# Weight, x and work tiles of a hybrid decoder layer laid on one grid of 512 bytes

## The chip, the cores and the metric

The kernel runs on one core of a Trainium2 chip. The metric is the time of one execution on the device, in microseconds. A core has five engines that run beside each other and meet through semaphores: TensorE (PE in the profile; PEld is its weight loading), VectorE (DVE), ScalarE (ACT), GpSimd (POOL) and SyncE (SP), which here only issues transfers. Engines work on SBUF, a memory of 128 partitions; a tile takes the same range of bytes in every partition, so the place of a tile is one start address, and addresses below are bytes within a partition. Products leave TensorE into PSUM.

## The reference

One decoder layer for 256 tokens of 2048 channels in float32: half a SwiGLU, a mixer of attention heads and S5 state-space channels side by side, half a SwiGLU again, and a last norm.

```python
h = h + 0.5 * swiglu(rmsnorm(h, ffn1_norm[l]), ffn1_w1[l], ffn1_w3[l], ffn1_w2[l])
proj = rmsnorm(h, mix_norm[l]) @ w_in[l]
...
a = nsa_mixer(q, kc, vc, ksl, vsl, kw, vw, gates, rel_bias, ...)
s = s5_mixer(u_ssm, ...)
h = h + jnp.concatenate([a, s], axis=-1) @ w_out[l]
h = h + 0.5 * swiglu(rmsnorm(h, ffn2_norm[l]), ffn2_w1[l], ffn2_w3[l], ffn2_w2[l])
return rmsnorm(h, final_norm)
```

Here swiglu(x) = (silu(x @ w1) * (x @ w3)) @ w2 with 5632 hidden columns. Its three matrices in two half-steps are most of the 337 MB that the layer reads, and most of its products.

## The kernel before

**Three passes for a float32 product.** A float32 number is split into hi (12 significant bits, type float32r) and lo (the rest). A product of x and w is three float32r matmuls that add up in PSUM: x hi with w hi, x hi with w lo, x lo with w hi. A matmul has a stationary operand, loaded as 128 x 128 weights into the array, and a moving operand that streams through it, here up to 512 columns.

**Row products** (`gemm_rows`, L173 to L175) have 128 tokens of x as the stationary operand (xh, xl) and 512 columns of the weight matrix as the moving one (whi, wlo); one k-tile of 128 rows takes 2 token tiles x 3 passes = 6 matmuls. For the product with w2 the hidden activations are the stationary operand; they lie in work tiles (wk). **Column products** (`cols_step`, L184 to L186) are the other way round: 128 columns of the weight are stationary and the 256 tokens move.

**Weights** arrive by two k-tiles: `wload` (L143) has SP load 512 KB into a raw tile, and `wtiles` (L151) splits it with one ScalarE instruction (L121, hi) and one VectorE instruction (L122, lo) into tiles whi and wlo, three buffers of each. After each pair of k-tiles `tick` advances the side work (S5 parameters, scan, attention) by a step. Instructions run on every engine in the order in which the program issues them, apart from a priority for the splits.

**Half-step** (`ffn`, L245): 11 blocks of 512 hidden columns. A block makes two row products over 16 k-tiles (w1, w3), the gate, four blocks of 4 k-tiles with w2 for the block before, and 8 transposes (L310) that turn the hidden rows into the stationary layout. In the last block of the second half-step the last two column blocks go one token tile after the other (`tail`, L259 to L269): their weights are split into work tiles ahead, and L265 to L267 are its row products, between work tiles only.

**Pools and addresses.** Tiles come from pools that lie one after the other in SBUF: const (L74), xt (x hi and lo, four buffers of 4096 bytes each), w (raw, whi, wlo: tiles of 2 x 536 float32 = 4288 bytes, of which 2 x 512 are mostly used, so that the second k-tile starts 2144 bytes on), work (49 buffers of 2048 bytes). The start addresses of the built program, taken modulo 512:

| tile | start modulo 512, before | bytes from one buffer to the next |
|---|---|---|
| xh, xl | 64 | 4096 |
| whi | 0, 192, 384 (second k-tile 96, 288, 480) | 4288 |
| wlo | 64, 256, 448 (second k-tile 160, 352, 32) | 4288 |
| work | 128 | 2048 |
| identity (in cst) | 128 | - |

Of the kernel before, what the change touches and what calls it, by code (L numbers as in the profile page):

```python
"""One hybrid decoder layer (macaron SwiGLU halves around parallel NSA attention heads and S5
channels) on one core.

Float32 products of the large projections run as three float32r passes over exact hi/lo parts
(x = hi + lo, 12 significant bits each): hi*hi + hi*lo + lo*hi. The norms' rsqrt factors are per
token, so the products take the unscaled rows and the factor comes in where they leave PSUM.
The three attention branches: with 256 tokens every 64-token block is among the chosen ones and
the window spans the whole sequence, so the chosen and the window branch are both full causal
attention, over their own keys and values.
"""  # L10
# [8 lines left out]
F32 = mybir.dt.float32  # L19
F32R = mybir.dt.float32r  # L20
# [9 lines left out]
T = 256  # L30
# [8 lines left out]
WMAX = 536  # L39

# [7 lines left out]
def _consts():  # L48
    """Constants that depend on shapes alone: identity, partition masks, T5 bucket one-hots."""
    p = np.arange(128)  # L50
    c = np.zeros((128, C_END), np.float32)
    c[:, C_ID:C_ID + 128] = np.eye(128)
    c[:, C_SEL:C_SEL + 32] = (p[:, None] % 32) == np.arange(32)
    c[:, C_EVEN] = (p // 16) % 2 == 0
    c[:, C_EVEN + 1] = (p // 16) % 2 == 1
    c[:, C_HALF] = p < 64
    c[:, C_HALF + 1] = p >= 64
    c[:, C_ROW:C_ROW + 8] = (p[:, None] // 16) == np.arange(8)
    dist = np.arange(256)
    large = 16 + (np.log(np.maximum(dist, 1) / 16.0) / math.log(8.0) * 16).astype(np.int64)  # L60
    bucket = np.where(dist < 16, dist, np.minimum(large, NB - 1))
    hot = np.zeros((NB, 384), np.float32)
    hot[bucket, 127 + dist] = 1.0
    return c, hot


def hymba_layer(tc, x, ffn1_norm, ffn1_w1, ffn1_w3, ffn1_w2, mix_norm, w_in,
# [6 lines left out]
    cp = ctx.enter_context(tc.tile_pool(name="const", bufs=1))  # L74
    xp = ctx.enter_context(tc.tile_pool(name="xt", bufs=4))
    wp = ctx.enter_context(tc.tile_pool(name="w", bufs=3))
    sp = ctx.enter_context(tc.tile_pool(name="work", bufs=49))
# [30 lines left out]
    def load_rows(c0, *srcs):  # L108
        """Parameter vectors as columns of 128, from column c0 of par."""
        rows = work([128, 128])  # L110
        n = 0
        for src, k in srcs:
            SP.dma_start(rows[n:n + k, :], src[0].rearrange("(r c) -> r c", c=128))
            n += k
        ps = tp_tile()
        PE.transpose(ps[:, :n], rows[:n, :], ident[:n, :n])
        V.tensor_copy(par[:, c0:c0 + n], ps[:, :n])

    def split(hi, lo, src, scale=1.0):
        """hi = fp32r(src * scale), lo = the rest; scale a number or a per-partition column."""  # L120
        S.activation(hi, src, AF.Copy if isinstance(scale, float) else AF.Identity, scale=scale)  # L121
        V.scalar_tensor_tensor(lo, src, scale, hi.bitcast(F32), op0=ALU.mult, op1=ALU.subtract)  # L122

# [19 lines left out]
    def wload(src, n):  # L143
        kq = src.shape[0] // 128
        raw = wp.tile([128, 2, WMAX], F32, name="raw", tag="raw", bufs=5)
        SP.dma_start(raw[:, :kq, :n], src.rearrange("(k p) n -> p k n", p=128))
        return raw

    ahead = []      # loads started before their product

    def wtiles(w, c0, n, k0=0, k1=None):  # L151
        """Yields (k-tile, hi, lo, index in the tile) over rows k0*128..k1*128 of w[:, c0:c0+n]."""
        k1 = w.shape[0] // 128 if k1 is None else k1
        for kb in range(k0, k1, 2):
            raw = ahead.pop(0) if ahead else wload(w[kb * 128:(kb + 2) * 128, c0:c0 + n], n)
            hi = wp.tile([128, 2, WMAX], F32R, name="whi", tag="whi")
            lo = wp.tile([128, 2, WMAX], F32R, name="wlo", tag="wlo")
            with tc.high_priority(offset=50):
                split(hi[:, :, :n], lo[:, :, :n], raw[:, :, :n])
            for i in range(2):  # L160
                yield kb + i, hi, lo, i
            tick()

    def gemm_rows(xs, w, c0, n, k0=0, k1=None, first=0, stop=None):
        """Natural layout: out[tt] = x[tt tokens, :] @ w[:, c0:c0+n]; xs maps a k-tile to (hi, lo)."""
        k1 = w.shape[0] // 128 if k1 is None else k1
        ps = [mm_tile() for _ in range(NT)]
        for kt, hi, lo, i in wtiles(w, c0, n, k0, k1):
            xh, xl = xs(kt)
            for tt in range(NT):  # L170
                t = slice(tt * 128, tt * 128 + 128)
                o = ps[tt][:, :n]
                PE.matmul(o, xh[:, t], hi[:, i, :n], start=kt == k0, stop=False)  # L173
                PE.matmul(o, xh[:, t], lo[:, i, :n], start=False, stop=False)  # L174
                PE.matmul(o, xl[:, t], hi[:, i, :n], start=False, stop=kt == k1 - 1)  # L175
        return ps

    def cols_step(ps, xs, kt, hi, lo, i, subs, last):
        """Transposed layout: ps[b][:, s*256:] += w[kt rows, 128 columns].T @ x.T for each block."""
# [16 lines left out]
    class Norm:  # L196
# [29 lines left out]
        def rstd(self, tts=(0, 1)):  # L226
            """(mean of squares + eps)^-0.5 from the exponent's half and three Newton steps."""
# [17 lines left out]
    def ffn(w1, w3, w2, xs, rstd, done, by_tokens=False):  # L245
        last = FF // 512 - 1

        def down(c, ht, ns):
# [8 lines left out]
            def tail(ns):  # L257
                """The last columns, one token tile after the other."""
# [70 lines left out]
    def exp_poly(o, z, shape):  # L329
        """exp on VectorE: z = k ln2 + r, a polynomial in r, 2^k put into the exponent bits."""  # L330
# [16 lines left out]
    def s5_prepare():  # L347
# [67 lines left out]
        def cmul(o_re, o_im, a, b, shape):  # L415
            """o = a * b, complex."""
            for o, (p, q), op in ((o_re, (0, 1), ALU.subtract), (o_im, (1, 0), ALU.add)):
                t = work(shape)
                V.tensor_tensor(o, a[0], b[p], ALU.mult)
                V.tensor_tensor(t, a[1], b[q], ALU.mult)  # L420
                V.tensor_tensor(o, o, t, op)
                yield

        # powers of e^{i phi}: fine n = 0..15, coarse 16 m, m = 0..7
# [17 lines left out]
        # B discretised, and B a for the earlier of two positions  # L442
# [8 lines left out]
        for hf in range(2):  # L451
            # C masked by group, as [states, 4 pairs x 32 ch]; C a; imaginary parts negated
# [23 lines left out]
            # B masked by group, as [(position, pair of two, 32 ch), states]; and the later  # L476
            # position's own input, Re(C B), as blocks of 16 x 16 channels
# [37 lines left out]
    def s5_table(i):  # L515
        """cos and sin of phi times the chunk, for four pairs."""
# [82 lines left out]
    rb = work([128, 2, T])          # the factor along the free axis, and times the scores' scale  # L599
# [10 lines left out]
    up = cp.tile([128, 2, 2, 128], F32, name="upad")       # [(position, pair of two, ch), half, pair, chunk]  # L610
# [3 lines left out]
    rho = cp.tile([128, 4, 128], F32, name="rho")          # the decay, zero where a pair's chunks start  # L614
    G.memset(rho, 0.0)
    ut = []          # the channels, [ch, two tiles, t]; doubled gelu output in the end
    hs = []          # (hi, lo) of the gelu'd channels, two tiles of 128 each
# [58 lines left out]
    def gelu2(o, y, shape):  # L676
        """2 gelu(y), the tanh form."""
# [7 lines left out]
    def compress(kc, pe, w1, b1):  # L685
        """The blocks' hidden layer, [hidden, (group, block)], gelu'd, doubled."""
# [15 lines left out]
        for lb in range(0, 32, 8):  # L702
            raw = wp.tile([128, 2, WMAX], F32, name="raw", tag="raw", bufs=5).rearrange("p a n -> p (a n)")
# [42 lines left out]
    kk, vv = [], []      # per group: [d, (chosen, window), s]; per branch: [s, s-tile, (group, d)]  # L746
# [188 lines left out]
    def last_rstd(tt):  # L935
        """The last norm's factor: ScalarE's root, its reciprocal, one Newton step."""
# [55 lines left out]
```

## Time and profile before

| | |
|---|---|
| median of 3 runs | 1884.26 us (1884.11 to 1884.59) |
| the profiled execution, first to last instruction | 1883.2 us |
| HBM read, written | 337.16 MB, 2.11 MB |
| mean DMA rate | 181 GB/s |
| raw loads of 512 KB for the half-steps | 528, landing 3.7 us after issue |

The profiled execution is told by its span; no other time of that execution is recorded. A group row gives line, engine, operation, output and inputs, shape and count, then busy microseconds in total, the mean of one in nanoseconds, and the idle time of the engine ahead of it with what ended that. A timeline row gives the start in microseconds, the duration, then the same names. Ends of matmuls are modelled and matmuls overlap, so what one costs is read from starts.

### The profile page before, as it was taken

The numbers are of one execution on the slowest core, as the hardware profiler recorded it, in microseconds if no ns is written. First come the engines' busy times: TensorE is split into PE (matmuls) and PEld (weight loads), VectorE is DVE, ScalarE is ACT, GpSimd is POOL, SyncE is SP. The second block draws the span as 40 slices with busy tenths as digits, with TensorE's granted clock in tenths as the row PEclk, the third lists the DMA queues.
The fourth block names the chain that finished last, engine by engine and source line by source line (L and its number), as shares of the span: only waits on it lengthen the run. The fifth ranks groups of instructions, "written<-read, shape, count | busy, mean of one in ns | idle before, by whom it ended". The sixth has DMA issues, their size and how long they took to land.

```text
span 1883.2 us, 24243 instructions
## 1 busy us (share of the span) xinstructions
PE 1857.8 (99%) x9365; PEld 1529.1 (81%) x9365; DVE 1197.2 (64%) x1636; ACT 833.5 (44%) x1081; POOL 14.7 (1%) x32
## 2 busy tenths in 40 slices
PE   8999999999999999999999999999999999999997
PEld 6888888888887888999887788888888888888886
DVE  5467666777877455789876565455555545545546
ACT  6444434333444443555437554443443443444344
POOL 0000000000000000000000000000000000000002
PEclk9999999999999999999999999999999999999999
DMA  7676665655565665554673456666666666666663
GB/s 237 186 206 187 184 188 181 189 169 178 179 191 183 190 186 185 168 152 142 180 213 113 132 176 208 188 182 188 190 182 187 190 183 186 187 187 185 187 187 128
DMA packets 193286, 340.84 MB, mean 181 GB/s; under 512 B 21034, under 2 KB 30868, under 8 KB 193172
## 3 DMA queue, kind: packets, MB, share of 16 engines
q1 hardware_dynamic: 193172, 339.31, 59.8%
q8 instruction: 73, 1.20, 0.3%
q14 instruction: 41, 0.34, 0.0%
HBM read 337.16 MB, written 2.11 MB: 180 GB/s over the span
## 4 chain that ended last, share of the span: by engine, by line
PE 52%; DVE 3%; issue 1%; ACT 0%; DMA 0%; ACTq 0%; SPq 0%; DVEq 0%
PE mm L173 14%; PE mm L174 14%; PE mm L175 14%; PE mm L184 1%; PE mm L185 1%; PE mm L186 1%; DVE wlo L122 1%; PE sd L631 1%; PE tp L795 1%; PE sd L819 1%; PE tp L310 1%; DVE wk L643 0%; PE tp L658 0%; PE tp L816 0%; DMA wk<-in_cmp_pe_v_dram 0%
## 5 line engine op out<-in xcount | busy, mean ns | idle before, releaser
L122 DVE SCALAR_TENSOR_TENSOR wlo<-raw,whi 128x1024 fp32r<-128x1024 f32 (+1 forms) x620 | 759.0, 1225 | 607.8 <-ACT whi L121 606.6
L121 ACT ACTIVATE whi<-raw 128x1024 fp32r<-128x1024 f32 (+1 forms) x620 | 657.4, 1060 | 953.4 <-PE mm L175 852.2
L173 PE MATMUL mm<-whi,xh 128*128 128x512 f32 x1536 | 609.1, 397 | 2.0 <-ACT whi L121 2.0
L174 PE MATMUL mm<-wlo,xh 128*128 128x512 f32 x1536 | 608.3, 396 | 0.0
L175 PE MATMUL mm<-whi,xl 128*128 128x512 f32 x1536 | 606.2, 395 | 0.0
L173 PEld LDWEIGHTS mm<-whi,xh 128*128 128x128 f32 x1536 | 288.8, 188 | 70.5 <-ACT whi L121 2.4
L175 PEld LDWEIGHTS mm<-whi,xl 128*128 128x128 f32 x1536 | 288.8, 188 | 67.3 <-DVE xl L122 0.4
L174 PEld LDWEIGHTS mm<-wlo,xh 128*128 128x128 f32 x1536 | 288.9, 188 | 66.0 <-issue 0.5
L173 PE MATMUL mm<-whi,wk 128*128 128x512 f32 x688 | 273.9, 398 | 0.0
L175 PE MATMUL mm<-whi,wk 128*128 128x512 f32 x688 | 272.2, 396 | 0.0
L174 PE MATMUL mm<-wlo,wk 128*128 128x512 f32 x688 | 271.1, 394 | 0.0
L175 PEld LDWEIGHTS mm<-whi,wk 128*128 128x128 f32 x688 | 129.2, 188 | 30.7
L174 PEld LDWEIGHTS mm<-wlo,wk 128*128 128x128 f32 x688 | 129.2, 188 | 30.0
L173 PEld LDWEIGHTS mm<-whi,wk 128*128 128x128 f32 x688 | 129.4, 188 | 29.5 <-issue 0.6
L255 DVE SCALAR_TENSOR_TENSOR h<-mm,h 128x512 f32<-128x512 f32 x176 | 113.6, 683 | 3.6 <-PE mm L267 2.8
L184 PE MATMUL mm<-xh,whi 128*128 128x256 f32 x384 | 112.1, 292 | 0.9 <-DVE wk L879 0.9
L185 PE MATMUL mm<-xh,wlo 128*128 128x256 f32 x384 | 108.2, 282 | 0.0
L186 PE MATMUL mm<-xl,whi 128*128 128x256 f32 x384 | 108.0, 281 | 0.0
L184 PEld LDWEIGHTS mm<-xh,whi 128*128 128x128 f32 x384 | 72.3, 188 | 2.8 <-issue 1.2
L185 PEld LDWEIGHTS mm<-xh,wlo 128*128 128x128 f32 x384 | 72.3, 188 | 0.7 <-issue 0.2
L186 PEld LDWEIGHTS mm<-xl,whi 128*128 128x128 f32 x384 | 72.3, 188 | 0.4 <-issue 0.4
L295 ACT ACTIVATE wk<-mm,rstd 128x512 f32<-128x512 f32 x44 | 29.9, 680 | 21.0 <-PE mm L175 20.9
(246 smaller groups left out, 997.5 us busy)
## 6 DMA issues: line engine op xcount, KB each, us to landing
raw<-in_ffn_w_dram SPq DMA_DIRECT2D x528, 512.0 KB, 3.7
raw<-in_w_in_dram SPq DMA_DIRECT2D x48, 512.0 KB, 3.7
raw<-in_w_out_dram SPq DMA_DIRECT2D x32, 512.0 KB, 3.7
raw<-in_w_in_dram SPq DMA_DIRECT2D x8, 536.0 KB, 4.1
raw<-in_glu_w_dram SPq DMA_DIRECT2D x8, 512.0 KB, 4.6
h<-in_x_dram SPq DMA_DIRECT2D x4, 512.0 KB, 8.0
raw<-in_cmp_w_k_dram SPq DMA_DIRECT2D x4, 512.0 KB, 4.3
raw<-in_cmp_w_v_dram SPq DMA_DIRECT2D x4, 512.0 KB, 6.8
```

Source lines behind the costliest of these rows:

```text
L121: S.activation(hi, src, AF.Copy if isinstance(scale, float) else AF.Identity, scale=scale)
L122: V.scalar_tensor_tensor(lo, src, scale, hi.bitcast(F32), op0=ALU.mult, op1=ALU.subtract)
L173: PE.matmul(o, xh[:, t], hi[:, i, :n], start=kt == k0, stop=False)
L174: PE.matmul(o, xh[:, t], lo[:, i, :n], start=False, stop=False)
L175: PE.matmul(o, xl[:, t], hi[:, i, :n], start=False, stop=kt == k1 - 1)
L184: PE.matmul(o, wh, xh, start=kt == 0 and q % 2 == 0, stop=False, skip_group_check=True)
L185: PE.matmul(o, wl, xh, start=False, stop=False, skip_group_check=True)
L186: PE.matmul(o, wh, xl, start=False, stop=last, skip_group_check=True)
L255: V.scalar_tensor_tensor(o, p, 0.5, o, op0=ALU.mult, op1=ALU.add)
L295: S.activation(sl, ps1[tt], AF.Silu, scale=rstd[:, tt:tt + 1])
L310: PE.transpose(ps[:, k, tt * 128:tt * 128 + 128], gates[tt][:, f:f + 128], ident)
L631: PE.matmul(ps[:, hf * 256:hf * 256 + 256], s5.bt[i // 2][ri][:, 2 * (i % 2) + hf, :], up[:, hf].rearrange("p a c -> p (a c)"), start=True ...
```

## The change

The pools change places: xt comes first, then w, then work, then a pool of its own for the raw tiles, and const last. whi and wlo tiles become rows of 1152 float32 (4608 bytes, nine times 512), and the second k-tile starts at 512 columns (2048 bytes) instead of 536, or at 536 for the one product with 536 columns. The room comes from the work pool, which has 48 buffers instead of 49. The diff also empties comment lines, left out here.

```diff
+WROW = 1152
...
-    cp = ctx.enter_context(tc.tile_pool(name="const", bufs=1))
     xp = ctx.enter_context(tc.tile_pool(name="xt", bufs=4))
     wp = ctx.enter_context(tc.tile_pool(name="w", bufs=3))
-    sp = ctx.enter_context(tc.tile_pool(name="work", bufs=49))
+    sp = ctx.enter_context(tc.tile_pool(name="work", bufs=48))
+    rp = ctx.enter_context(tc.tile_pool(name="raw", bufs=5))
+    cp = ctx.enter_context(tc.tile_pool(name="const", bufs=1))
...
-        raw = wp.tile([128, 2, WMAX], F32, name="raw", tag="raw", bufs=5)
+        raw = rp.tile([128, 2, WMAX], F32, name="raw", tag="raw")
...
-            hi = wp.tile([128, 2, WMAX], F32R, name="whi", tag="whi")
-            lo = wp.tile([128, 2, WMAX], F32R, name="wlo", tag="wlo")
+            s = max(n, 512)
+            hi, lo = (wp.tile([128, WROW], F32R, name=k, tag=k)[:, :2 * s].rearrange("p (k n) -> p k n", k=2)
+                      for k in ("whi", "wlo"))
```

In the built program xh, xl, whi, wlo and work tiles now all start at 128 modulo 512, and the second k-tile of a weight tile too, except with 536 columns (224). The identity starts at 64. The instructions and their order are the same on every engine; the splits write one run of 1024 where they wrote two of 512, and some waits for a freed work tile go to another reader, as the tiles rotate through 48 buffers.

More of the change, by code (lines that the diff above doesn't have):

```diff
@@ L702, in compress @@
         for lb in range(0, 32, 8):
-            raw = wp.tile([128, 2, WMAX], F32, name="raw", tag="raw", bufs=5).rearrange("p a n -> p (a n)")
+            raw = rp.tile([128, 2, WMAX], F32, name="raw", tag="raw").rearrange("p a n -> p (a n)")
             SP.dma_start(raw[:, :1024].rearrange("p (l n) -> p l n", n=128),
```

## The prediction

> **What bounds the kernel now.** I read the page's engine shares first, then the clock row of the slices, then the groups by line with different shapes kept apart, and last the timeline of TensorE in three places.
>
> ```profile
> span 1883.2 us, 24243 instructions
> PE 1857.8 (99%) x9365; PEld 1529.1 (81%) x9365; DVE 1197.2 (64%) x1636; ACT 833.5 (44%) x1081; POOL 14.7 (1%) x32
> ...
> PEclk9999999999999999999999999999999999999999
> ```
>
> TensorE is busy for 99% of the span, and the clock it was granted is full in every slice. No other engine is over 64%. So there is almost no wait to remove: the time can change only if a product itself takes more or less of TensorE's time. The groups say which products count:
>
> ```profile
> L173 PE MATMUL mm<-whi,xh 128*128 128x512 f32 x1536 | 609.1, 397 | 2.0 <-ACT whi L121 2.0
> L174 PE MATMUL mm<-wlo,xh 128*128 128x512 f32 x1536 | 608.3, 396 | 0.0
> L175 PE MATMUL mm<-whi,xl 128*128 128x512 f32 x1536 | 606.2, 395 | 0.0
> L173 PE MATMUL mm<-whi,wk 128*128 128x512 f32 x688 | 273.9, 398 | 0.0
> L175 PE MATMUL mm<-whi,wk 128*128 128x512 f32 x688 | 272.2, 396 | 0.0
> L174 PE MATMUL mm<-wlo,wk 128*128 128x512 f32 x688 | 271.1, 394 | 0.0
> ```
>
> These are the row products: 3 x (1536 + 688) = 6672 of them, each 512 columns wide, with activations (xh, xl, or wk for the hidden rows) as the stationary operand and weights (whi, wlo) as the moving one. A mean of 394 to 398 ns is not what one costs, because they are pipelined: the next starts long before the last has ended. The cost is the spacing of the starts, read from the timeline. One block of 512 hidden columns in the second half-step lies between these rows:
>
> ```profile
> 1297.45 1.03 PE L310 MATMUL tp<-cst,wk 128*128 128x128 f32 x8
> 1298.24 0.48 PE L173 MATMUL mm<-whi,wk 128*128 128x512 f32 x1
> 1298.56 0.39 PE L174 MATMUL mm<-wlo,wk 128*128 128x512 f32 x1
> ...
> 1365.21 1.03 PE L310 MATMUL tp<-cst,wk 128*128 128x128 f32 x8
> ```
>
> Between two transposes a block has 288 row products: 2 projections x 16 k-tiles x 2 token tiles x 3 passes = 192, and 4 column blocks x 4 k-tiles x 2 x 3 = 96. Without the first, whose start follows a transpose, 287 products take 1365.21 - 1298.56 = 66.65 us, **0.2322 us each**. At 6672 of them that is 1549 of the 1883 us. One nanosecond on the spacing is worth 6.7 us.
>
> **The one place where the trace already has aligned operands.** Before, an x tile starts at byte 64 of a grid of 512 bytes, a work tile at 128, whi at 0, 192 or 384, wlo at 64, 256 or 448, and the second half of a weight tile 96 further (2144 bytes). So moving and stationary operands are hardly ever a multiple of 512 apart, and hardly anywhere is a moving operand aligned with both the weights loaded while it streams and its own. The exception is the tail of the last block (L265 to L267): there the weights were split into work tiles of 2048 bytes, the hidden rows are work tiles too, and every operand starts at byte 128 of the grid. Its groups and its starts:
>
> ```profile
> L267 PE MATMUL mm<-wk 128*128 128x512 f32 x16 | 6.2, 390 | 0.0
> L266 PE MATMUL mm<-wk 128*128 128x512 f32 x16 | 6.2, 390 | 0.0
> L265 PE MATMUL mm<-wk 128*128 128x512 f32 x16 | 6.2, 389 | 0.0
> ```
>
> ```profile
> 1855.00 0.40 PE L173 MATMUL mm<-whi,wk 128*128 128x512 f32 x1
> ...
> 1862.68 0.39 PE L265 MATMUL mm<-wk 128*128 128x512 f32 x1
> ...
> 1863.38 0.39 PE L265 MATMUL mm<-wk 128*128 128x512 f32 x1
> ...
> 1864.76 0.39 PE L265 MATMUL mm<-wk 128*128 128x512 f32 x1
> ...
> 1873.38 0.39 PE L267 MATMUL mm<-wk 128*128 128x512 f32 x1
> ```
>
> From 1864.76 to 1873.38 there are 38 steps (13 triples of L265, L266, L267): 8.62 / 38 = **0.2268 us**. The same shape, type and order of passes as L173 to L175, and 5.4 ns less. The first nine of the tail, 1862.68 to 1864.76, still take 2.08 / 9 = 0.2311. The obvious other reason is that the tail is quiet: no weights come in any more. But the 33 misaligned products just ahead, 1855.00 to 1862.68, take 7.68 / 33 = 0.2327, and the windows over both show no transfers in either:
>
> ```profile
> 1855.00:1862.00 7.00, 7.00 (x32) 5.65 (x31) 5.59 (x7) 4.48 (x9) 2.56 (x2) 1.00 0.00 0
> 1864.70:1872.00 7.30, 7.30 (x33) 6.03 (x33) 3.22 (x8) 3.60 (x9) 4.42 (x5) 1.00 0.00 0
> ```
>
> The columns are PE, PEld, DVE, ACT and POOL busy, the clock, the share of DMA and GB/s. DMA is at 0.00 in both. DVE works 80% of the first window and 44% of the second, yet the ordinary block above, with DVE and the loads at their usual load, has 0.2322, no more than the first window. So the spacing does not follow the neighbours' work; it follows the operands. That is my reason.
>
> **The change, part by part.**
>
> *Row products.* After, xh, xl, whi, wlo and every work tile start at byte 128 of the grid, and the second half of a weight tile is 2048 bytes on: exactly the tail's condition, for all 6672. 6672 x 0.0054 = **-36.0 us**. Not all get it. After an interruption nine products may run at 0.2311 before the spacing settles, as in the tail. The transposes in the half-steps and of the norms interrupt in groups of eight and four:
>
> ```profile
> L310 PE MATMUL tp<-cst,wk 128*128 128x128 f32 x176 | 23.2, 273 | 0.0
> L215 PE MATMUL tp<-cst,h 128*128 128x128 f32 x96 | 16.0, 300 | 0.0
> ```
>
> That is 176 / 8 = 22 and 96 / 4 = 24 times; with as many again for the side work of the mixer stage (an estimate) 90 times nine products at 4.3 ns more than settled: 90 x 9 x 0.0043 = 3.5 us at most. I take +2, since many stretches are shorter than nine.
>
> *Column products* (L184 to L186, 256 wide, weights stationary):
>
> ```profile
> L184 PE MATMUL mm<-xh,whi 128*128 128x256 f32 x384 | 112.1, 292 | 0.9 <-DVE wk L879 0.9
> L184 PE MATMUL mm<-wk,whi 128*128 128x256 f32 x64 | 18.5, 289 | 0.0
> L861 PE MATMUL mm<-whi,xh 128*128 128x280 f32 x32 | 9.4, 294 | 0.0
> L861 PE MATMUL mm<-whi,xh 128*128 128x256 f32 x32 | 9.0, 281 | 0.0
> ...
> 953.52 0.28 PE L184 MATMUL mm<-xh,whi 128*128 128x256 f32 x1
> ...
> 958.86 0.28 PE L184 MATMUL mm<-xh,whi 128*128 128x256 f32 x1
> ```
>
> Fifteen triples in 5.34 us: 0.1187 each. 3 x (384 + 64) = 1344 of them, and 3 x (32 + 32) = 192 row products of 256 or 280 columns, are aligned too, except the second half of the eight 536-column tiles, which stay 96 bytes off. The trace has no aligned one. Bounds: no gain, and the whole 5.4 ns of the tail, 1536 x 0.0054 = 8 us; a loss of as much is the third end. I take -2, a quarter of the gain, because these products alternate with the side work of the mixer stage, for which TensorE sometimes waits.
>
> *Constants moved to the end.* The identity goes from byte 128 to 64 of the grid, so the 176 transposes L310 (identity against work tiles) lose the alignment they had. Priced by the tail again, 176 x 0.0054 = 1 us either way; I take 0.
>
> *48 work buffers for 49.* The order of instructions on every engine stays the same; only which earlier reader a new tile waits for shifts by one. Who waits most for a freed work tile, and who keeps TensorE waiting:
>
> ```profile
> POOL wk L696 <- PE tp L658: 543.0, 1, 543.0
> POOL wk L479 <- PE mm L174: 173.4, 2, 106.2
> ...
> PE tp L658 <- DVE xs L651: 3.5, 5, 0.8
> ```
>
> The first two (us in total, times, longest) are GpSimd, which runs far ahead and fills a tile as soon as it is free; those waits cost nothing, since the users come later. The third is TensorE's longest wait in total after the start, and it is for data, not for a tile. So a lost buffer is hidden by distance: between two uses of one buffer lie 47 others. If that cover were gone somewhere, five waits of 0.7 us, as long as that row's, would be +3.5 us. Between 0 and that; I take 0.
>
> *The split's output* (L121, L122) is one run of 1024 in place of two of 512:
>
> ```profile
> GB/s 237 186 206 187 184 188 181 189 169 178 179 191 183 190 186 185 168 152 142 180 213 113 132 176 208 188 182 188 190 182 187 190 183 186 187 187 185 187 187 128
> ...
> L122 DVE SCALAR_TENSOR_TENSOR wlo<-raw,whi 128x1024 fp32r<-128x1024 f32 (+1 forms) x620 | 759.0, 1225 | 607.8 <-ACT whi L121 606.6
> L121 ACT ACTIVATE whi<-raw 128x1024 fp32r<-128x1024 f32 (+1 forms) x620 | 657.4, 1060 | 953.4 <-PE mm L175 852.2
> ```
>
> It is hidden: twelve products at 0.2268 are 2.72 us per weight tile, against 1.2 on DVE and 1.1 on ACT. What is late next? The loads: 512 KB per 2.72 us is 193 GB/s, and the first of the page's 40 slices moved 237. So a faster TensorE is still fed.
>
> **Sum.** -36.0 + 2 - 2 + 0 = -36. The profiled execution spans 1883.2 us and the median of the runs is 1884.26, 1.1 more for what lies around the span. 1883.2 - 36 + 1.1 = **1848 us**, -1.9%.
>
> **Rivals.**
>
> *Address plays no part.* Then the tail is fast for another reason, such as having no splits ahead of it, and nothing changes: 1884. The Trainium skill speaks for it: "TensorE: Matmul & The Clock Gate", section "Step-by-step: what each phase is for", gives TensorE two independent SBUF read ports, so loading the next weights takes nothing from the running product; by that rule alignment is worth 0 us here. The 0.2327 and 0.2268 on the two sides of 1862.68 speak against it. The Trainium skill's same page, section "Back-to-back issue gap", has about 216 ns for 512 columns; by it alone the estimate would reach 6672 x 0.0162 = 108 us less, which no row here supports, the aligned tail included.
>
> *Half of it.* The weights' buffers lie 4608 bytes apart, x tiles 4096, and the rate may depend on more than the residue by 512. If the bulk settles midway between 0.2322 and 0.2268: 18 us, 1866. For it: the groups L173 to L175 with the same alignment differ by 2 to 4 ns. Against: in the tail the operands lie at many different multiples of 512 and all 38 steps are alike.
>
> *Slower: aligned tiles collide with the splits.* All tiles that ACT and DVE write now share one residue with what TensorE reads. The tail's first three products, 1862.68 to 1863.38, run beside the last split on DVE, whose two instructions reach to 1863.11:
>
> ```profile
> 1861.83 1.28 DVE L122 SCALAR_TENSOR_TENSOR wk<-raw,wk 128x512 fp32r<-128x512 f32 x2
> ```
>
> They take 0.70 / 3 = 0.2333. If that is the aligned rate beside splits, and splits run through the whole kernel, 6672 x 0.0011 = +7 us: 1891. It decides the sign from a spacing of 0.2322 + 0.0006 on. Against: products four to nine are slow without any split beside them, so the nine look like settling.
>
> **Numbers.** 0.2% is 3.8 us, about what a measurement of this kernel can tell from no change. Forecast 0.72, with a range of its own from 1840 (column products gain all 8 us, no loss by settling) to 1858 (settling and other stages eat 10); half of it 0.12; no part 0.08; collisions 0.08. Faster 0.84, same 0.08, slower 0.08. The range for 8 in 10 takes in most of the half case: 1838 to 1867.
>
> **What would show it.** Right: L173 to L175 at a mean of about 390 ns, like L265 to L267; the L310 rows of the second half-step a shorter way apart: a block, now 1365.21 - 1297.45 = 67.76 us, takes 67.76 - 288 x 0.0054 = 66.2; TensorE still 99% busy. Column products under 0.118 show the second term. Wrong: blocks at 67.8 (no part), at 67.0 (half), over 67.9 (collisions); or new idle time of TensorE in the mixer stage behind a work tile.

## The result, and the profile after

The changed kernel takes 1851.91 us (median of 4 runs, 1851.02 to 1852.75) against 1884.18 for the kernel before in the same series (4 runs, 1883.27 to 1884.59): a ratio of 0.9828, 95% interval 0.9814 to 0.9842. The profiled execution spans 1850.2 us, 33.0 less than the one before; its own time is 1852.75.

The page of the kernel after, engine shares and clock:

```profile
span 1850.2 us, 24247 instructions
PE 1826.3 (99%) x9365; PEld 1530.0 (83%) x9365; DVE 1196.9 (65%) x1636; ACT 834.2 (45%) x1081; POOL 14.7 (1%) x32
...
PEclk9999999999999999999999999999999999999999
```

TensorE's busy time fell by 31.5 us and its clock was full before and is full now; no other engine's busy time moved by more than 1 us. The groups by shape of the kernel after say where (line 173 has become 176, and so on; then the column products):

```profile
L176 PE MATMUL mm<-whi,xh 128*128 128x512 f32 x1536 | 601.4, 392 | 2.0 <-ACT whi L123 2.0
L177 PE MATMUL mm<-wlo,xh 128*128 128x512 f32 x1536 | 600.1, 391 | 0.0
L178 PE MATMUL mm<-whi,xl 128*128 128x512 f32 x1536 | 599.8, 391 | 0.0
L176 PE MATMUL mm<-whi,wk 128*128 128x512 f32 x688 | 270.3, 393 | 0.0
L178 PE MATMUL mm<-whi,wk 128*128 128x512 f32 x688 | 268.4, 390 | 0.0
L177 PE MATMUL mm<-wlo,wk 128*128 128x512 f32 x688 | 268.0, 390 | 0.0
L187 PE MATMUL mm<-xh,whi 128*128 128x256 f32 x384 | 112.7, 294 | 0.9 <-DVE wk L882 0.9
```

Every group of row products is 4 to 6 ns shorter in its mean; the six together went from 2640.8 to 2608.0 us, 32.8 less. The first group of column products went the other way, 292 to 294 ns. The timeline of the kernel after, at the ends of one block and at the start of the tail:

```profile
1277.47 1.04 PE L313 MATMUL tp<-cst,wk 128*128 128x128 f32 x8
...
1343.68 1.04 PE L313 MATMUL tp<-cst,wk 128*128 128x128 f32 x8
...
1829.80 0.39 PE L268 MATMUL mm<-wk 128*128 128x512 f32 x1
1830.03 0.39 PE L269 MATMUL mm<-wk 128*128 128x512 f32 x1
1830.26 0.39 PE L270 MATMUL mm<-wk 128*128 128x512 f32 x1
1830.48 0.39 PE L268 MATMUL mm<-wk 128*128 128x512 f32 x1
```

A block of 288 row products now takes 66.21 us instead of 67.76. The tail has no slow start any more: its first three take 0.68 us, 0.2267 each, where before nine products passed until that was reached. What came ahead of it is now aligned as well.

### The profile page after: what moved, and what is told of

Same layout as the page of the kernel before. It is cut to its first block, busy times and chain, and to the rows that moved or that the text cites. A ratio compares the mean times of both kernels' runs of the same rounds, so it can differ in the third digit from the quotient of the medians.

```text
span 1850.2 us, 24247 instructions
## 1 busy us (share of the span) xinstructions
PE 1826.3 (99%) x9365; PEld 1530.0 (83%) x9365; DVE 1196.9 (65%) x1636; ACT 834.2 (45%) x1081; POOL 14.7 (1%) x32
## 4 chain that ended last, share of the span: by engine, by line
PE 52%; DVE 3%; issue 1%; DMA 1%; ACT 0%; ACTq 0%; SPq 0%; DVEq 0%
PE mm L176 14%; PE mm L178 14%; PE mm L177 14%; PE mm L187 1%; PE mm L188 1%; PE mm L189 1%; PE sd L634 1%; DVE wlo L124 1%; PE tp L798 1%; PE sd L822 1%; PE tp L313 1%; DVE wk L646 0%; PE tp L661 0%; DMA raw<-in_w_in_dram 0%; PE tp L819 0%
## 5 line engine op out<-in xcount | busy, mean ns | idle before, releaser
L124 DVE SCALAR_TENSOR_TENSOR wlo<-raw,whi 128x1024 fp32r<-128x1024 f32 (+1 forms) x620 | 759.1, 1225 | 577.2 <-ACT whi L123 576.1
L123 ACT ACTIVATE whi<-raw 128x1024 fp32r<-128x1024 f32 (+1 forms) x620 | 658.0, 1061 | 922.1 <-PE mm L178 814.5
L176 PE MATMUL mm<-whi,xh 128*128 128x512 f32 x1536 | 601.4, 392 | 2.0 <-ACT whi L123 2.0
L177 PE MATMUL mm<-wlo,xh 128*128 128x512 f32 x1536 | 600.1, 391 | 0.0
L178 PE MATMUL mm<-whi,xl 128*128 128x512 f32 x1536 | 599.8, 391 | 0.0
L176 PE MATMUL mm<-whi,wk 128*128 128x512 f32 x688 | 270.3, 393 | 0.0
L178 PE MATMUL mm<-whi,wk 128*128 128x512 f32 x688 | 268.4, 390 | 0.0
```

## The experiments

Theories: **alignment** (a product is fast when its moving and stationary operands lie a multiple of 512 bytes apart), **regularity** (it is fast when the distance stays the same from product to product, whatever it is), and a **longer or shorter grid** than 512.

### The distance by itself

`sweep`, a kernel of TensorE products alone, 24 for each pair of tiles (one execution):

```diff
+    for n in (512, 256):
+        for k in range(16):
+            for j in range(4):
+                for r in range(24):
+                    PE.matmul(ps[:, r % 4, :n], st[j], mv[k][:, 8 * k:8 * k + n], start=True, stop=True)
```

> Leaves out the whole layer: TensorE alone runs 24 products each for 16 distances (moving tiles mva to mvp, 32 bytes further each, 0 to 480 modulo 512) and 4 stationary tiles (sta to std, 512 bytes apart), first 512 and then 256 columns wide; the output is a copy of a sum that means nothing. Theory of alignment: of the 16 distances, a multiple of 512 (mva) has the smallest spacing at 512 columns, 0.2267 us, and most others have 0.229 to 0.236, whatever the stationary tile. Theory of regularity (what costs time is that the distance changes from product to product, not its value): all 64 groups alike, near 0.2267. Theory of a longer grid: the four stationary tiles differ by some ns at the same distance. For 256 columns: alignment as in the kernel after, about 0.120, and others on both sides of it (0.113 to 0.124).

Rows of its timeline (start, duration, tiles, count). The spacing at one distance is the step from one sta row to the next, divided by 4 x 24 = 96:

```profile
34.46 5.77 PE L93 MATMUL acc<-mvb,sta 128*128 128x512 f32 x24
56.87 5.67 PE L93 MATMUL acc<-mvc,sta 128*128 128x512 f32 x24
78.85 5.77 PE L93 MATMUL acc<-mvd,sta 128*128 128x512 f32 x24
...
168.53 5.75 PE L93 MATMUL acc<-mvh,sta 128*128 128x512 f32 x24
190.92 5.61 PE L93 MATMUL acc<-mvi,sta 128*128 128x512 f32 x24
196.37 5.60 PE L93 MATMUL acc<-mvi,stb 128*128 128x512 f32 x24
201.81 5.60 PE L93 MATMUL acc<-mvi,stc 128*128 128x512 f32 x24
207.25 5.60 PE L93 MATMUL acc<-mvi,std 128*128 128x512 f32 x24
212.69 5.77 PE L93 MATMUL acc<-mvj,sta 128*128 128x512 f32 x24
...
369.15 3.03 PE L93 MATMUL acc<-mva,sta 128*128 128x256 f32 x24
380.65 3.00 PE L93 MATMUL acc<-mvb,sta 128*128 128x256 f32 x24
...
437.44 2.92 PE L93 MATMUL acc<-mvg,sta 128*128 128x256 f32 x24
448.35 3.00 PE L93 MATMUL acc<-mvh,sta 128*128 128x256 f32 x24
```

At 512 columns: 32 bytes (mvb) 22.41 / 96 = 0.2334 us, 64 (mvc) 21.98 / 96 = 0.2290, 224 (mvh) 0.2332, 256 (mvi) 21.77 / 96 = **0.2268**. The 32-byte steps not shown between these lie from 0.2332 to 0.2342. At distance 0 (mva) the three tiles behind the warm-up have 0.2267. The pattern then repeats: mvj (288) is mvb again, mvk (320) is mvc. **The grid is 256 bytes, not 512.** The four stationary tiles, 512 bytes apart, are alike to 0.01 us in 24 products, so nothing longer counts. Regularity alone falls: each of these distances was constant, and most are as slow as the kernel before.

At 256 columns the order is another: distance 0 takes 11.50 / 96 = 0.1198 us, 192 (mvg) 10.91 / 96 = 0.1136, the other steps of 32 bytes 0.117 to 0.120. **Aligned is among the slowest there**, and the change put all column products on it.

### One distance for all products, but not 0

`shift64`:

```diff
-            hi, lo = (wp.tile([128, WROW], F32R, name=k, tag=k)[:, :2 * s].rearrange("p (k n) -> p k n", k=2)
+            hi, lo = (wp.tile([128, WROW], F32R, name=k, tag=k)[:, 16:16 + 2 * s].rearrange("p (k n) -> p k n", k=2)
```

> The changed kernel with every whi and wlo operand 64 bytes further in its tile: all distances between x or work tiles and weights are again the same for all products, but 64 modulo 512 instead of 0. Alignment: row products back at about 0.232, 1884 us. Regularity: 0.227 as after, 1852 us. A good value by chance: the kernel before had 0.2262 in the products whose next stationary operand lay 64 beyond the moving one, so below 0.227 and 1848 us is possible.

1862.42 us (2 runs), ratio 0.9886 (0.9857 to 0.9914). This is none of the three numbers. The median step between the starts of its row products is 0.2290, the sweep's value at 64; the kernel follows the sweep at a distance that no theory had singled out. (The 0.2262 of the kernel before had come from a sequence of changing distances.) By the sum of all starts the row products take 1539.3 us, 12.2 more than in the changed kernel, and the column products, now at 192, give 4.1 back (168.8 against 172.9).

### Two distances in turn

`half96`:

```diff
-            s = max(n, 512)
+            s = WMAX
```

> The changed kernel with the second k-tile of a weight tile at 2144 bytes again instead of 2048, so half of the row products are 96 bytes off the grid. Alignment: that half at 0.232 and the other at 0.227, about 1868 us. Regularity within runs of six products: 1852 to 1857 us.

1887.67 us (8 runs), ratio **1.0018** (1.0007 to 1.0029): slower than the kernel before, though half of its products are aligned. The groups and one block of it:

```profile
L177 PE MATMUL mm<-wlo,xh 128*128 128x512 f32 x1536 | 609.7, 397 | 0.0
L176 PE MATMUL mm<-whi,xh 128*128 128x512 f32 x1536 | 609.6, 397 | 2.0 <-ACT whi L123 2.0
```

```profile
1299.44 1.03 PE L313 MATMUL tp<-cst,wk 128*128 128x128 f32 x8
...
1367.35 1.03 PE L313 MATMUL tp<-cst,wk 128*128 128x128 f32 x8
```

A block takes 67.91 us. By the starts in the trace, without the steps of 260 ns and more in which something comes between, the aligned half has 0.2314 and the other 0.2341, where the sweep, with each distance held, has 0.2267 and 0.2334. In the kernel before, the same two halves have 0.2314 and 0.2330: the aligned half gained nothing. So six products in a row are too few to reach the fast spacing. Both theories fall in their simple form: alignment counts, and it must last.

`sweep2` measures that by itself, and finer distances:

```diff
+    for c, k in zip("qrstuv", (1, 2, 3, 6, 12, 24)):
+        run(c, 512, [96 * (r // k % 2) for r in range(144)])
+    run("w", 512, [256 * (r // 6 % 2) for r in range(144)])
```

> Leaves out the whole layer: TensorE alone runs products with one stationary tile and moving tiles mva to mvp at 0, 4, 8, 12, 16, 24, 40, 48, 56, 72, 80, 112, 144, 176, 208 and 240 bytes, 36 each, 512 and then 256 columns wide; then, at 512 columns, 144 products each that change between 0 and 96 bytes every 1, 2, 3, 6, 12 and 24 products (mvq to mvv), and between 0 and 256 every 6 (mvw). If the grid of 256 is all there is: 0.2267 at 0 alone, 0.228 to 0.236 elsewhere; a distance below 16 bytes could behave as 0. Memory (settling over about nine products): changes every 1 to 6 products give 0.231 to 0.234, every 24 about 0.231, falling with the length of a run. No memory: all six near the mean of 0.2267 and 0.2336, 0.2302. mvw at 0.2267 if only the residue by 256 counts.

Its timeline, 144 products a row:

```profile
214.30 33.28 PE L87 MATMUL acc<-mvq,st 128*128 128x512 f32 x144
247.43 33.52 PE L87 MATMUL acc<-mvr,st 128*128 128x512 f32 x144
280.79 33.68 PE L87 MATMUL acc<-mvs,st 128*128 128x512 f32 x144
314.30 33.68 PE L87 MATMUL acc<-mvt,st 128*128 128x512 f32 x144
347.82 33.60 PE L87 MATMUL acc<-mvu,st 128*128 128x512 f32 x144
381.26 33.44 PE L87 MATMUL acc<-mvv,st 128*128 128x512 f32 x144
414.54 32.84 PE L87 MATMUL acc<-mvw,st 128*128 128x512 f32 x144
```

Steps between starts, divided by 144: changes every 1, 2, 3, 6, 12 and 24 products give 0.2301, 0.2317, 0.2327, **0.2328**, 0.2322 and 0.2311. The mean of the two held distances is 0.2300. Runs of three and six lie 2.7 ns above it, runs of 24 begin to come back, and a change at every product costs just the mean, which memory did not lead me to expect. Inside the runs of twelve, the starts after a return to distance 0 are 233, 236, 224, 231, 236, 228, 233, 230 ns apart (in some returns a nanosecond off) and then 227. The tail before the change has the same eight steps, to the nanosecond, from 1862.91 to 1864.76, behind one more of 233. So a change of distance is enough for settling, with no other engine at work here. Other products in between do it as well: in the changed kernel, behind the transposes at 1277.47 and a first step of 312 ns, nine steps of 224 to 236 ns pass before 227. mvw, between 0 and 256 every six, has 0.2267 once its first eight steps are over. Of the fine distances at 512 columns (4 to 240 bytes) none is faster than 0.2289; 4 bytes have 0.236, so a small offset is not a small loss.

### Is 512 needed, and which part of the change is?

`grid256`: `s = 576` for `s = max(n, 512)`, so that the second k-tile starts at 2304 bytes.

> The changed kernel with the second k-tile of a weight tile at 2304 bytes instead of 2048: half of the operands lie on odd multiples of 256 from the x and work tiles, and the 536-column tiles come onto the grid. If the grid is 256: as after, 1852 us, row products 0.227. If it is 512, as the change has it: as the run with 96 bytes, 1888 us.

1852.78 us (2 runs), 0.9831 (0.9803 to 0.9860): as after. Half of the operands sit on odd multiples of 256, and a block takes 66.21 us as well.

`rowonly`, the old pools with the new weight tiles: they and the work tiles start at 0, x tiles at 64.

```diff
+WROW = 1152
...
-    sp = ctx.enter_context(tc.tile_pool(name="work", bufs=49))
+    sp = ctx.enter_context(tc.tile_pool(name="work", bufs=48))
...
-            hi = wp.tile([128, 2, WMAX], F32R, name="whi", tag="whi")
-            lo = wp.tile([128, 2, WMAX], F32R, name="wlo", tag="wlo")
+            s = max(n, 512)
+            hi, lo = (wp.tile([128, WROW], F32R, name=k, tag=k)[:, :2 * s].rearrange("p (k n) -> p k n", k=2)
+                      for k in ("whi", "wlo"))
```

> The kernel before with only the weight tiles' shape changed (4608 bytes, second k-tile at 2048) and 48 work buffers; pools in their old order. Weights and work tiles start at 0 modulo 512, x tiles at 64: the products with w2 are aligned, those with x are 64 off. Alignment: products of wk at 0.227, those of xh at 0.232, saving 2064 x 5 ns = 10 us, 1874 us. Regularity: all at 0.227, 1852 us.

1879.29 us (8 runs), 0.9973 (0.9962 to 0.9985). Its groups part exactly by stationary operand:

```profile
L175 PE MATMUL mm<-whi,xh 128*128 128x512 f32 x1536 | 610.5, 398 | 2.0 <-ACT whi L122 2.0
L176 PE MATMUL mm<-wlo,xh 128*128 128x512 f32 x1536 | 609.2, 397 | 0.0
...
L175 PE MATMUL mm<-whi,wk 128*128 128x512 f32 x688 | 270.2, 393 | 0.0
L176 PE MATMUL mm<-wlo,wk 128*128 128x512 f32 x688 | 268.3, 390 | 0.0
```

The wk products, aligned, are as short as after (393, 390); the xh products stay long (398, 397), a nanosecond over before. The moving tiles are the same in both: the distance to the stationary operand decides, not where the moving one lies. The gain is half of what alignment was to give, because the moving weights now lie 64 bytes below x, that is 192 modulo 256, where the sweep (moving minus stationary) has 0.2332, worse than the 0.2322 of the scattered distances. By the sums of starts the wk products take 10.7 us less than before (472.3 against 483.0), which is the 10 that alignment was to give, and the xh and xl products 5.6 more (1083.1 against 1077.5).

`poolsonly`, the new pools and 48 work buffers with the old weight tiles:

> The changed kernel with the weight tiles' old shape (4288 bytes, second k-tile at 2144), pools in the new order and 48 work buffers. The distances scatter again as before: alignment has 0.232 and 1884 us; if the order of the pools or the place of the constants did something by itself, the time moves without the tiles' shape.

1883.60 us (8 runs), 0.9996 (0.9985 to 1.0007): nothing. The order of the pools, the place of the constants and the missing work buffer have no price of their own that can be measured, at least while the distances scatter.

### The column products

`colshift`: the changed kernel, with 64 bytes more for the weights of the column products.

```diff
-    def wtiles(w, c0, n, k0=0, k1=None):
+    def wtiles(w, c0, n, k0=0, k1=None, sh=0):
...
-            hi, lo = (wp.tile([128, WROW], F32R, name=k, tag=k)[:, :2 * s].rearrange("p (k n) -> p k n", k=2)
+            hi, lo = (wp.tile([128, WROW], F32R, name=k, tag=k)[:, sh:sh + 2 * s].rearrange("p (k n) -> p k n", k=2)
...
-        for kt, hi, lo, i in wtiles(w, c0, 512):
+        for kt, hi, lo, i in wtiles(w, c0, 512, sh=16):
...
-        for kt, hi, lo, i in wtiles(win, 1536 + 512 * br, 256 + n):
+        for kt, hi, lo, i in wtiles(win, 1536 + 512 * br, 256 + n, sh=16):
```

> The changed kernel with the weight tiles of the column products alone (and of the mixed key and value product) 64 bytes further, so that the moving x lies 192 modulo 256 from the stationary weights; row products stay aligned. By the sweep (0.1133 at 192 against 0.1200 at 0) 1344 products gain up to 6.7 ns: 1843 us; by the column products of the run with 64 bytes (0.1174 against 0.1212) 5 us: 1847. If the side work of the mixer stage sets the pace there: 1852, no gain.

1850.46 us (2 runs), 0.9819 (0.9791 to 0.9848): between the second and the third of the expected numbers. To tell it from the changed kernel, both were timed once more on one chip:

> The same kernel as in colshift, timed beside the changed kernel on one chip. If the column products' gain (about 2 us by the spans, 1848.1 against 1850.2) is real, the two times lie 1.5 to 3 us apart, about 0.1%, and both 1.7 to 1.9% under the kernel before; if it is noise between calls, they agree within 0.5 us.

> The changed kernel again, as the partner of colshift5: 1851.9 us, 1.7% under the kernel before.

1850.67 us (5 runs, 1849.56 to 1852.35) against 1852.98 (4 runs, 1851.87 to 1854.31); ratios to before 0.9820 (0.9806 to 0.9833) and 0.9831 (0.9818 to 0.9844). They lie 2.3 us apart in the median, with ranges that just overlap. The groups of colshift show it more plainly:

```profile
L187 PE MATMUL mm<-xh,whi 128*128 128x256 f32 x384 | 111.2, 290 | 0.9 <-DVE wk L882 0.9
L188 PE MATMUL mm<-xh,wlo 128*128 128x256 f32 x384 | 107.3, 279 | 0.0
L189 PE MATMUL mm<-xl,whi 128*128 128x256 f32 x384 | 107.1, 279 | 0.0
```

In the changed kernel these three rows have 294, 283 and 283 ns, in both of its traces; the row products are unchanged. So the version with two distances, 0 for rows and 64 for columns, is the fastest of the study, by an amount near the edge of what these runs tell. By the sums of starts the column products take 169.9 us (colshift) and 169.2 (colshift5), against 172.9 and 173.4 in the two traces of the changed kernel: 3 to 4 of the 9 us that the sweep promised.

The rest is missing because at this distance the column products have two lasting spacings, not one. Of some 1225 steps between column products (none of 150 ns or more), 588 are 113 or 114 ns and 569 are 117 to 119 in colshift; in colshift5, the same kernel, 755 and 398. One stretch of the program shows both. These rows are its second product and the product behind its last, in colshift and then in colshift5:

```profile
961.85 0.28 PE L188 MATMUL mm<-xh,wlo 128*128 128x256 f32 x1
...
971.63 0.28 PE L187 MATMUL mm<-wk,whi 128*128 128x256 f32 x1
```

```profile
962.16 0.28 PE L188 MATMUL mm<-xh,wlo 128*128 128x256 f32 x1
...
971.58 0.28 PE L187 MATMUL mm<-wk,whi 128*128 128x256 f32 x1
```

The 83 steps take 9.78 / 83 = 0.1178 us in one execution and 9.42 / 83 = 0.1135 in the other. So this is not slow settling: most stretches take one of the two rhythms within a few products and keep it. What decides which one is not shown. Part of the gain also goes into a wait (total us, times, longest), here of colshift:

```profile
PE tp L661 <- DVE xs L654: 4.6, 7, 1.0
```

The changed kernel has 2.9 us, 5 times, in that row of its waits; the side work of the mixer stage is now sometimes late.

## Why the prediction was right, point by point

- **The bound.** TensorE was the bound and stayed it, 99% busy, with the clock full. Nothing else came late at the faster pace: loads and splits fed 66.21 us blocks as they had fed 67.76 us ones.
- **Row products, -36 with 2 for settling.** Right in mechanism and size. The sum of all starts in the two traces gives 1560.5 us before and 1527.1 after for them, 33.4 less, against a forecast of 34. The block was forecast at 66.2 and is 66.21. The tail of 48 products was a fair sample, because the sweep shows that the residue, and nothing longer, decides. That the neighbours' work plays no part also holds: in the sweep no other engine works beside the products, and most misaligned distances still have 0.2333. Only the length of the grid was off: 512 bytes are enough, but 256 are all that is needed, which the tail could not tell.
- **Settling over nine products.** It was argued from one place in the trace; sweep2 repeats eight of these nine steps, to the nanosecond, without any other engine at work. As a correction to this change it was also right in size: over the steps of row products under 260 ns, the kernel after lies 2.2 us above the settled 226.7, and the term was +2. That settling can decide a whole change I had not seen. In half96 the 3336 aligned products in runs of six gained nothing against the same products before, the other half lost 1 ns each, and the kernel became slower.
- **Column products, -2.** The term with the wrong sign. I carried the tail's 5.4 ns over to 256 columns as the nearest row, with a loss of the same size as the other bound. The sweep has 0.1198 aligned against 0.1136 to 0.120 elsewhere, and by all starts the column products took 0.4 us more after than before. This 2.4 us and the 0.6 of the row term make up the 3.0 by which the span of 1850.2 missed the forecast's 1847.2, as far as one execution tells: another of the changed kernel (after5) spans 1851.8. The rest of the 3.9 us between 1848 and 1851.9 is not the kernel's work but an error in the sum. Its 1.1 us around the span was the median of the runs less the span of one execution. Where both are on record for the same run, they lie 1.7 to 2.1 us apart before (1884.27 and 1882.2 in one) and 2.3 to 2.6 after (1852.75 and 1850.2).
- **Constants, 48 buffers, the splits' output: 0 each.** poolsonly, with all but the last of these, is at 0.9996; the splits' means are 1225 and 1061 ns after, 1225 and 1060 before.
- **Rival: address plays no part.** Fallen. The Trainium skill ("TensorE: Matmul & The Clock Gate", section "Step-by-step: what each phase is for") describes the two SBUF read ports of TensorE as independent. The traces do not agree with the conclusion I drew from it, that the addresses are free: in rowonly the same moving tiles give 393 ns against one stationary operand and 398 against another.
- **Rival: half of it.** Fallen as a rule of longer grids: the four stationary tiles of the sweep are alike.
- **Rival: collisions with the splits.** Fallen. Splits run through the whole kernel, and the blocks have the aligned spacing all the same. The tail's first three at 0.2333 were settling: sweep2 repeats the second and the third of them, 233 and 236 ns, on an otherwise idle core.

Why the distance matters is not shown. That the loading of the next stationary operand meets the streaming of the moving one in SBUF would fit, since their distance counts; the runs do not reach into that.

## What to carry to other kernels

When TensorE is 99% busy, look at the spacing of its starts, not at its busy share, and look for one place in the kernel where the same product runs at another pace: here 48 products beside the 6672 gave the size of the whole change. Tile sizes that are not a multiple of the grid scatter the operands' distances; padding them costs a few hundred bytes a tile. But a partial cure can be worse than none, and another shape can want another distance: sweep it in a kernel of its own before laying out the pools.

## What the hardware showed that I had not expected

- The grid is 256 bytes: 0.2268 us at a distance of 256 as at 0, for float32r products of 512 columns, and a kernel on that grid as fast as on 512.
- At 256 columns the best of the 32-byte steps is 192 (0.1136 us), and 0 (0.1198) is among the slowest. A distance of 16 bytes in sweep2 has 0.1133, so 192 is not the only good one.
- At 256 columns and a distance of 192, one stretch of the same kernel ran at 0.1178 us in one execution and at 0.1135 in another.
- Two distances in turn can cost more than the mean of the two: 0 and 96 every six products take 0.2328 where the mean is 0.2300; in the whole kernel that was 1.0018 of before.
- A distance of 4 bytes is as bad as any: 0.236 us in sweep2.
